# Projections with tokens as weights: 512 columns in place of 256, single weight and stage tiles, halves of the values, first heads fetched by the sync queue

## The chip, the cores and the metric

One core of one Trainium2 chip runs the kernel. The metric is the device time of one execution in microseconds (us). A core has TensorE (PE, matrix products from SBUF into PSUM; PEld is its loading of stationary operands), VectorE (DVE), ScalarE (ACT), GpSimd (POOL) and SyncE (SP); here SP does nothing but issue transfers (DMA). "SPq" and "ACTq" in a row are the queue instructions of those engines.

## The reference

One layer of a streaming encoder over 2048 tokens of width 1024, in float32.

```python
mod = silu(c) @ w_ada + b_ada                     # shifts, scales, gates: 6 x 1024
h = rmsnorm(x, g_norm1) * (1 + sc1) + sh1
q_sb, k_sb, v_sb, q_ca, k_ca, v_ca = split(h @ w_in)   # 512 columns each, 8 heads of 64
o_sb = stick_breaking_attention(q_sb, k_sb, v_sb)
o_ca = chunked_relpos_attention(rmsnorm(q_ca, g_q), rmsnorm(k_ca, g_k), v_ca, rel_bias)
x = x + gt1 * (concat(o_sb, o_ca) @ w_o)
x = x + gt2 * (relu(h2 @ w1) ** 2 @ w2)           # h2: second norm, shift and scale
```

SB names the stick-breaking heads and CA the chunked heads. CA queries and keys are normalised per head (a sum of squares over 64 columns), SB ones are not.

## The kernel before

**Products.** Each float32 operand is split into a high and a low part (`split`: ScalarE rounds a copy, another engine subtracts it from the original). A product is three matmuls (`mm3`, L202): high by high, high by low, low by high. "Stationary" is the operand that PE holds as weights, "moving" the one that streams through in columns.

**Pieces and jobs.** The 3072 columns of `w_in` are 12 pieces of 256: 0 and 1 are q_sb, 2 and 3 k_sb, 4 and 5 v_sb, 6 and 7 q_ca, 8 and 9 k_ca, 10 and 11 v_ca. Tokens are in four blocks of 512 (tb 0 to 3). A job is (f, piece, tb), where f only tells several loads of one piece apart. The startup (L437 to L506) computes the SB pieces 2, 0, 1 for block 3 in one loop over the 8 slices k of the contraction, while it computes the first columns of `mod` on VectorE (`ada_column`, L260) and normalises block 3. Then the list `jobs` (L522) is run, one after the other, by `run_job` (L538), to which the last job is left until the first attention heads' loads are issued (L1036). The SB pieces that the list lacks are projected later, during the attention (`pf` in the traces, weights `fw` read back from `scr_w`).

**Two forms of projection** (`project`, L310). For SB queries and keys the weights (128x128) are stationary and 512 tokens move; the result is tile `pq`. For CA queries and keys and all values 128 tokens of `ht` are stationary and the 256 columns of the piece move; the result is tile `pt`, and two token groups share one PSUM bank. A job of the second form is 96 matmuls. For CA it goes on with the norm per head (squares `csq` on ScalarE, sums `cv` on VectorE, the root on GpSimd), a scaled copy `qh` (VectorE), and four transposes on PE into `px`, evicted with the factor `gqk_s` into a stage tile `st` and stored to `scr_q` or `scr_k`. Values go through a stage tile `sv` to `scr_v`. Jobs of this kind are run behind their matmuls by small clocks (`Later`: a job added with n ticks runs after n PSUM groups).

**Weights** (`load_w`, L282). A raw piece (1 MB, tile `wr`, 3 buffers) is copied into `wh` by ScalarE and subtracted into `wl` by GpSimd, in eight slices; both are double buffered as whole pieces (8 slices each). `keep_w` (L305) stores them to `scr_w` for those pieces that the attention needs again.

**Norms.** `start_norm(tb, wait)` (L402) squares and adds block tb (`nsqa`, `nsaa`), and after `wait` ticks sums over partitions on PE (`pva`), takes the root, and after more ticks spreads it on PE (`pra`) and multiplies block tb by it (L412). `end_norm` (L418) applies scale and shift and splits into `ht`.

**Order.** From job 7 on (`ORDERED`) every engine keeps the order of the program text (those operations all show as line L42); between the startup and job 7 a scheduler orders ScalarE, VectorE and GpSimd. PE's order is that of the text throughout. The queue for the first attention heads' pieces is ScalarE's (`ldq = act`, L601).

Of the kernel before, what the change touches and what calls it, by code (L numbers as in the profile page):

```python
# [79 lines left out]
def encoder_kernel(ctx, tc, xT, c, g1, g2, w_in, gqk, bias, w_o, w1, w2, w_ada, b_ada, out):  # L80
# [127 lines left out]
    def store_qk(kind, ca, ps, pl, pair, tb, nm, g=None):  # L208
        st = pl.tile([P, 2, TB], F32R, tag="st", name=f"st{nm}")
# [6 lines left out]
        sp.dma_start(scr_k[at].rearrange("l d t -> d l t") if kind else scr_q[at], st.bitcast(F32))  # L216
# [21 lines left out]
    SBQK, CAQK, VALS = (2, 3, 0, 1), (6, 7, 8, 9), (4, 5, 10, 11)  # L238

    pa, er = ctx.enter_context(ExitStack()), ctx.enter_context(ExitStack())
    if True:
        xp = er.enter_context(tc.tile_pool(name="xp", bufs=KT + 2, side="right"))
        adaw = er.enter_context(tc.tile_pool(name="adaw", bufs=4, side="right"))
        adap = er.enter_context(tc.tile_pool(name="adap", bufs=1, side="right"))
# [5 lines left out]
        wp = pa.enter_context(tc.tile_pool(name="wp", bufs=2))  # L252
        ppc = er.enter_context(tc.tile_pool(name="ppC", bufs=1, space=PSUM))
        pp = Banks(zb, zb, db, zb, zb, db)

        cb = adap.tile([P, D], F32, name="cb")
        cg = adap.tile([P, D], F32, name="cg")
# [8 lines left out]
        parts = []  # L266

        def ada(j):
            wa = adaw.tile([P, D], F32, tag="wa", name=f"wa{j}")
            sp.dma_start(wa, w_ada[j * P : (j + 1) * P, :])  # L270
            behind.add(2, lambda: ada_column(j, wa))
# [5 lines left out]
        def load_raw(half, piece, q=None):  # L277
            wr = ring.tile([P, KT, CW], F32, tag="r8", name=f"wr{half}_{piece}")
            (q or sp).dma_start(wr, w_in[piece])
            return wr  # L280

        def load_w(half, piece, q=None, wr=None, parts=None):  # L282

            if wr is None:
                wr = load_raw(half, piece, q or sp)
            wh = wp.tile([P, KT, CW], F32R, tag="wh", name=f"wh{half}_{piece}")
            wl = wp.tile([P, KT, CW], F32R, tag="wl", name=f"wl{half}_{piece}")

            def low(k):
                pool.tensor_tensor(wl[:, k], wr[:, k], wh[:, k].bitcast(F32), op=ALU.subtract)  # L290

            for k in (slice(0, KT // 2), slice(KT // 2, KT)):
                act.copy(wh[:, k], wr[:, k])
                for kk in (slice(k.start, k.start + 2), slice(k.start + 2, k.stop)):
                    if parts is None:
                        low(kk)
                    else:
                        parts.append(lambda kk=kk: low(kk))
            if parts is not None:
                parts.append(lambda: behind.add(2, lambda: keep_w(half, piece, wh, wl)))  # L300
            elif q is None:
                keep_w(half, piece, wh, wl)
            return wh, wl

        def keep_w(half, piece, wh, wl):  # L305
            if half in (0, 2) and piece not in CAQK:
                for l, w in enumerate((wh, wl)):
                    sp.dma_start(scr_w[piece,][:, :, l, :], w.bitcast(F32))

        def project(piece, tb, ht, wh, wl):  # L310

            grp, hf = divmod(piece, 2)
            kind, ca = grp % 3, grp // 3
            nm = f"{piece}_{tb}"
            if not ca and kind < 2:
                for n in range(2):
                    ps = pp.tile([P, TB], F32, tag="ps", name=f"pq{nm}_{n}")
                    cl = slice(n * P, (n + 1) * P)
                    for k in range(KT):
                        mm3(ps, wh[:, k, cl], wl[:, k, cl], ht[k][:, 0, :], ht[k][:, 1, :], k == 0, k == KT - 1)  # L320
                    store_qk(kind, 0, ps, stp, hf * 2 + n, tb, f"{nm}_{n}")
                    yield
                return
            if kind < 2:
                qh = stp.tile([P, 4, CW], F32, tag="qh", name=f"qh{nm}", bufs=2)
            for t2 in range(2):
                ps = pp.tile([P, TB], F32, tag="ps", name=f"pt{nm}_{t2}")
                for tt in range(2):
                    tl = slice((2 * t2 + tt) * P, (2 * t2 + tt + 1) * P)
                    for k in range(KT):  # L330
                        mm3(
                            ps[:, tt * CW : (tt + 1) * CW], ht[k][:, 0, tl], ht[k][:, 1, tl],
                            wh[:, k, :], wl[:, k, :], k == 0, k == KT - 1,
                        )
                if kind == 2:
                    store_v(ca, ps, stp, hf, tb, t2, f"{nm}_{t2}")
                    yield
                    continue
                sq = np_.tile([P, TB], F32, tag="nsq", name=f"csq{nm}_{t2}")
                act.activation(sq, ps, AF.Square)  # L340
                v = np_.tile([P, NH], F32, tag="cv", name=f"cv{nm}_{t2}")
                dve.tensor_reduce(v, sq.rearrange("p (h d) -> p h d", d=HD), axis=AX.X, op=ALU.add)
                dve.tensor_scalar(v, v, 1.0 / HD, EPS, op0=ALU.mult, op1=ALU.add)
                y = np_.tile([P, NH], F32, tag="cy", name=f"cy{nm}_{t2}")
                t = np_.tile([P, NH], F32, tag="ct", name=f"ct{nm}_{t2}")
                rsqrt(y, v, t)
                def scale(t2=t2, ps=ps, y=y):
                    dve.tensor_tensor(
                        qh[:, 2 * t2 : 2 * t2 + 2, :].rearrange("p t (h d) -> p (t h) d", d=HD),
                        ps.rearrange("p (e d) -> p e d", d=HD),  # L350
                        y.unsqueeze(2).to_broadcast([P, NH, HD]),
                        op=ALU.mult,
                    )

                later.add(2 if osp is sp else 1, scale)
                if t2 == 1:
                    def turn(n):
                        pt = pp.tile([P, TB], F32, tag="ps", name=f"px{nm}_{n}")
                        for i in range(4):
                            pe.transpose(pt[:, i * P : (i + 1) * P], qh[:, i, n * P : (n + 1) * P], ident)  # L360
                        store_qk(
                            kind, 1, pt, stp, hf * 2 + n, tb, f"{nm}_{n}", gqk_s[:, kind : kind + 1],
                        )

                    later.add(4, lambda: turn(0))
                    later.add(4, lambda: turn(1))
                yield

        def prepare_wo(n):
# [3 lines left out]
            def rest():  # L373
                hi = stp.tile([P, KT, P], F32R, tag="st", name=f"woh{n}")
                lo = stp.tile([P, KT, P], F32R, tag="st", name=f"wol{n}")
# [4 lines left out]
            behind.add(2, rest)  # L380
# [12 lines left out]
        xts, hts, ws = {}, {}, {}  # L393
# [8 lines left out]
        def start_norm(tb, wait=3):  # L402
# [3 lines left out]
            def second():  # L406
                dg = norm_rstd(np_, pp, acc, tg)

                def third():
                    r = norm_spread(pp, dg, tg)  # L410
                    for x in xts[tb]:
                        dve.tensor_tensor(x, x, r, op=ALU.mult)  # L412
# [1204 lines left out]
```

## Time and profile before

| what | value |
|---|---|
| three executions | 2698.66, 2701.07, 2701.13 us, median 2701.07 |
| profiled execution | 2697.3 us |
| its span, from the first to the last instruction | 2695.4 us |
| mean granted TensorE clock | 0.992 |
| projections, to the first attention scores on PE | 438.6 us |

A timeline row is: start in us, duration in us, engine, line, operation, output tile <- input tiles, shape, how many in a run, and in brackets the idle time before it and what ended it. A group's row gives busy us and mean ns, or minimum, median and maximum ns of one. Matmul ends are modelled, so in a stream the distance of starts is what a matmul costs.

### The profile page before, as it was taken

What the parts mean: (1) busy time and instruction counts of PE and PEld (TensorE: products, weight loads), DVE (VectorE), ACT (ScalarE), POOL (GpSimd) and SP (SyncE); (2) the same over time, 40 slices, a digit from 0 to 9 for tenths busy, and PEclk for the clock granted to TensorE, in tenths of its full rate; (3) what the DMA queues carried; (4) which work ended last, traced back from release to release, by engine and by line L of the source; (5) the groups of instructions that cost most, each with busy time, mean ns of one, the idle gap of its engine ahead of it and who ended that gap; (6) DMA issues with size and microseconds to landing.
All of it is one profiled execution on the core that took longest, in us unless ns stands there. A gap on an engine that the chain in (4) does not pass through costs nothing. (4 is left out here: it accounts for less than half of the span.)

```text
span 2695.4 us, 42695 instructions
## 1 busy us (share of the span) xinstructions
PE 2618.6 (97%) x14192; PEld 2231.0 (83%) x14192; DVE 1881.3 (70%) x3191; ACT 1516.9 (56%) x2926; POOL 1013.1 (38%) x1264
## 2 busy tenths in 40 slices
PE   6999999899999999999999999999999999999999
PEld 5899998778778987778777888878888888888887
DVE  6435555788789978989757778767857555655565
ACT  5323444788688878878644444456544444444443
POOL 5454365576466756777522233200001323200000
PEclk9999999999999999999999999999999999999999
DMA  9869977978878688766667776786675444465574
GB/s 343 296 257 336 379 300 213 275 243 256 273 250 253 202 261 253 235 191 203 205 235 275 253 277 240 275 327 212 227 269 183 149 157 145 149 242 188 203 265 156
DMA packets 265580, 650.36 MB, mean 241 GB/s; under 512 B 29200, under 2 KB 65040, under 8 KB 255632
## 3 DMA queue, kind: packets, MB, share of 16 engines
q1 hardware_dynamic: 264576, 645.55, 70.0%
q10 hardware_dynamic: 784, 2.10, 0.3%
q8 instruction: 112, 1.84, 0.3%
q14 instruction: 108, 0.88, 0.1%
HBM read 456.16 MB, written 191.37 MB: 240 GB/s over the span
## 5 line engine op out<-in xcount | busy, mean ns | idle before, releaser
L42 PE MATMUL ps<-oph,opv 128*128 128x512 f32 x2688 | 612.3, 389 | 1.7 <-ACT opv L42 1.5
L42 PE MATMUL ps<-h,opw 128*128 128x512 f32 x2664 | 607.0, 390 | 2.2 <-DVE cx L42 2.0
L42 PEld LDWEIGHTS ps<-oph,opv 128*128 128x128 f32 x2688 | 503.8, 188 | 108.3 <-ACT opv L42 2.3
L42 PEld LDWEIGHTS ps<-h,opw 128*128 128x128 f32 x2664 | 500.3, 188 | 108.5 <-DVE cx L42 3.1
L42 POOL TENSOR_TENSOR b<-b,p 128x512 f32<-128x512 f32 (+1 forms) x320 | 359.7, 1124 | 188.3 <-DVE p L42 167.8
L42 DVE TENSOR_TENSOR wtl<-wt,wth 128x512 fp32r<-128x512 f32 (+3 forms) x544 | 289.9, 544 | 50.4 <-ACT wth L42 48.1
L42 ACT CAST wth<-wt 128x512 fp32r<-128x512 f32 (+3 forms) x544 | 257.6, 484 | 115.2 <-PE wt L42 99.6
L42 DVE TENSOR_TENSOR oph<-hw,oph 128x512 fp32r<-128x512 f32 x224 | 156.1, 697 | 220.3 <-ACT oph L42 220.3
L42 PE MATMUL pt<-wh,ht 128*128 128x256 f32 x1664 | 304.3, 284 | 1.7 <-DVE qh L42 1.7
L42 POOL TENSOR_TENSOR ts<-w 128x512 f32<-128x512 f32 x32 | 44.9, 1403 | 681.5 <-DMA w<-in_w_dram 310.0
L42 ACT CAST oph<-hw 128x512 fp32r<-128x512 f32 x224 | 139.3, 622 | 282.8 <-PE ps L42 267.3
L42 DVE TENSOR_TENSOR_SCAN p<-z,p,zero 128x512 f32<-128x512 f32 x192 | 245.9, 1281 | 34.1 <-ACT z L42 28.9
L42 PEld LDWEIGHTS pt<-wh,ht 128*128 128x128 f32 x1664 | 260.8, 192 | 1.9 <-ACT st L42 1.9
L42 PE MATMUL pt<-wl,ht 128*128 128x256 f32 x832 | 235.3, 283 | 0.0
L42 PE MATMUL acc<-wth,v 128*128 128x512 f32 (+3 forms) x544 | 223.0, 414 | 0.0
L42 ACT ACTIVATE b<-z 128x512 f32<-128x512 f32 (+1 forms) x320 | 171.6, 536 | 63.2 <-PE z L42 45.9
L42 POOL TENSOR_TENSOR e<-e,cols 128x640 f32<-128x640 f32 (+4 forms) x128 | 143.0, 1121 | 145.6 <-DVE cols L42 86.7
L42 PE MATMUL z<-k,q 128*128 128x512 f32 (+3 forms) x640 | 186.3, 373 | 9.9 <-DVE p L42 7.2
L42 PE MATMUL acc<-wtl,v 128*128 128x512 f32 (+3 forms) x544 | 187.1, 350 | 0.0
L42 PE MATMUL wt<-ident,b 128*128 128x128 f32 x1088 | 173.3, 275 | 6.7 <-DVE cols L42 5.1
L42 DVE TENSOR_TENSOR opw<-w,opw 128x512 fp32r<-128x512 f32 x127 | 100.4, 793 | 112.7 <-ACT opw L42 112.6
L42 ACT ACTIVATE z<-z 128x512 f32<-128x512 f32 (+1 forms) x320 | 170.7, 533 | 0.0
(222 smaller groups left out, 4644.5 us busy)
## 6 DMA issues: line engine op xcount, KB each, us to landing
hw<-scr_hid SPq DMA_DIRECT2D x112, 512.0 KB, 4.0
v<-scr_v SPq DMA_DIRECT2D x136, 256.0 KB, 3.8
k<-scr_k SPq DMA_DIRECT2D x268, 128.0 KB, 4.1
w<-in_w_dram SPq DMA_DIRECT2D x64, 512.0 KB, 5.2
hw<-scr_s SPq DMA_DIRECT2D x64, 512.0 KB, 4.7
q<-scr_q SPq DMA_DIRECT2D x124, 256.0 KB, 5.2
fw<-scr_w SPq DMA_DIRECT2D x28, 1024.0 KB, 7.0
wa<-in_w_ada_dram SPq DMA_DIRECT2D x48, 512.0 KB, 7.0
```

The lines of the kernel that those rows point to most:

```text
L42: return lambda *x, **y: self.tc.keep_in_program_order(f(*x, **y))
```

## The change

- Pieces from 4 on are taken in pairs, 512 columns at once (`w_rest`, a second view of `w_in` made on the host). 128 tokens are stationary as before and 512 columns move; one token group fills one PSUM bank. The banks are now four for projections (`pp`) and two for norms and transposes (`pq`).
- Split weights lie in nine single tiles, each the high and low part of one slice of 512 columns (or two slices of 256). The low part is made by VectorE in place of GpSimd. During the last token group of a key `pump` refills each tile after PE's last use of it.
- Staging is six single tiles `st`; a value group is written as two halves of 256 columns, two token groups to a store. `qh` is six tiles of 128x512. The scale that writes it runs two projections later (`scale_last`), and the four transposes of a job come 3 and 4 groups later.
- `start_norm` multiplies by the learned scale as well (one instruction a slice), and `end_norm` adds the shift on ScalarE and makes the low part on VectorE: 8 and 8 instructions, where it was 16 and 8. Its position for block 2 is two groups later.
- All engines and SP keep the order of the text from the start on.
- The list of jobs is new (below); piece 3 for block 2 is loaded and split once more.
- `gqk` is loaded behind the first six stores and scaled on VectorE after the first half of (0,3,3); pieces 2 and 3 are stored to `scr_w` by ScalarE's queue.
- The last job is (1,4,1) with 512 columns; `ldq` is SP's queue in program order.

```diff
-        VALS = (4, 5, 10, 11)
+    CAQK, VALS = (6, 8), (4, 10)
+    WT = 9
...
-            dve.tensor_tensor_reduce(cb, wa, cs, 1.0, bcol[:, j : j + 1], ALU.mult, ALU.add, m)
+            dve.tensor_tensor_reduce(wa, wa, cs, 1.0, bcol[:, j : j + 1], ALU.mult, ALU.add, m)
...
+        def weight_parts(key, m):
+            f, p = key
+            w = w_tile(f"{f}_{p}_{m}")
+            wts.setdefault(key, []).append(w)
...
+            split(hi, lo, src)
...
+        def pump():
+            while coming and free[0]:
+                weight_parts(*coming.pop(0))
+        def scale_last():
+            for x in scales:
+                x[0] += 1
+            while scales and scales[0][0] == 2:
+                scales.pop(0)[1]()
...
-            for t2 in range(2):
-                ps = pp.tile([P, TB], F32, tag="ps", name=f"pt{nm}_{t2}")
-                for tt in range(2):
-                    tl = slice((2 * t2 + tt) * P, (2 * t2 + tt + 1) * P)
-                    for k in range(KT):
-                        mm3(
-                            ps[:, tt * CW : (tt + 1) * CW], ht[k][:, 0, tl], ht[k][:, 1, tl],
-                            wh[:, k, :], wl[:, k, :], k == 0, k == KT - 1,
-                        )
+            for tt in range(4):
+                ps = pp.tile([P, TB], F32, tag="ps", name=f"pt{nm}_{tt}")
+                tl = slice(tt * P, (tt + 1) * P)
+                if last and tt == 3:
+                    pump()
+                for k in range(KT):
+                    mm3(ps, ht[k][:, 0, tl], ht[k][:, 1, tl], *weight_of(key, k), k == 0, k == KT - 1)
+                    if last and tt == 3:
+                        free[0] += 1
+                        pump()
+                scale_last()
...
-                    for x in xts[tb]:
-                        dve.tensor_tensor(x, x, r, op=ALU.mult)
+                    for k, x in enumerate(xts[tb]):
+                        dve.scalar_tensor_tensor(x, x, aff[:, 0, k : k + 1], r, op0=ALU.mult, op1=ALU.mult)
...
-                norm_apply(0, xts[tb][k], k, ht, np_, f"a{tb}")
+                b = mod[:, k : k + 1]
+                act.activation(ht[k][:, 0, :], x, AF.Identity, bias=b)
+                dve.scalar_tensor_tensor(
+                    ht[k][:, 1, :], x, b, ht[k][:, 0, :].bitcast(F32), op0=ALU.add, op1=ALU.subtract
+                )
...
-        jobs = [(0, 3, 3), (0, 6, 3), (0, 3, 2), (0, 6, 2), (2, 2, 2), (0, 0, 2), (0, 1, 2)]
-        jobs += [(0, p, t) for p in seq[5:10] for t in (3, 2)]
-        jobs += [(0, 10, 3), (0, 11, 3), (0, 10, 2), (0, 11, 2)]
-        jobs += [(1, p, t) for p, t in ((4, 1), (6, 1), (7, 1), (6, 0), (7, 0), (8, 1), (8, 0), (9, 1), (9, 0), (5, 1))]
+        jobs = [(0, 3, 3), (0, 6, 3), (0, 6, 2), (2, 3, 2), (2, 2, 2), (0, 8, 3), (0, 8, 2), (2, 0, 2), (2, 1, 2)]
+        jobs += [(0, p, t) for p in (4, 10) for t in (3, 2)]
+        jobs += [(1, p, t) for p, t in ((6, 1), (6, 0), (8, 1), (8, 0), (4, 1))]
...
-        start_norm(2, 1)
+        start_norm(2, 2, 2)
...
-        ldq = act
+        ldq = osp
```

Three places show how instructions move. In the rows a name carries piece, block and group (`pq0_3_3_1` is f 0, piece 3, block 3, second half; `pt0_6_3_0` f 0, piece 6, block 3, token group 0).

PE's order at the end of (0,3,3) and the start of (0,6,3), before:

```order
L42 MATMUL pq3_3_0_759<-ht3_7_397,wh0_3_674 128x512 x2
L42 MATMUL pq3_3_0_759<-ht3_7_397,wl0_3_675 128x512
L42 MATMUL pva2_788<-ones_261,nsaa2_726 128x1 x4
L42 MATMUL pq3_3_1_804<-ht3_0_390,wh0_3_674 128x512 x2
L42 MATMUL pq3_3_1_804<-ht3_0_390,wl0_3_675 128x512
```

And PE's order there after:

```order
L42 MATMUL pq0_3_3_1_785<-ht3_5_392,w0_3_2_673 128x512 x3
L42 MATMUL pq0_3_3_1_785<-ht3_6_393,w0_3_3_676 128x512 x3
L42 MATMUL pq0_3_3_1_785<-ht3_7_394,w0_3_3_676 128x512 x3
L42 MATMUL pva2_838<-ones_261,nsaa2_729 128x1 x4
L42 MATMUL pt0_6_3_0_858<-w0_6_0_786,ht3_0_387 128x512 x3
L42 MATMUL pt0_6_3_0_858<-w0_6_1_789,ht3_1_388 128x512 x3
```

The sum over partitions for block 2 (`pva2`) stood between the two halves of (0,3,3); it now stands behind the second half, ahead of (0,6,3), whose matmuls read one weight tile for each slice.

VectorE's order around the end of the norm of block 2, where `xt2` and `ht2` are that block, `cv` the sums of a CA norm and `qh` the scaled copy, before:

```order
L412 TENSOR_TENSOR xt2_7_696<-xt2_7_696,pra2_833 128x512
L148 TENSOR_TENSOR ht2_981<-xt2_0_682,ht2_981 128x512
L148 TENSOR_TENSOR ht2_981<-xt2_1_684,ht2_981 128x512
L342 TENSOR_REDUCE cv6_3_0_900<-csq6_3_0_898 128x8
L148 TENSOR_TENSOR ht2_981<-xt2_2_686,ht2_981 128x512
L343 TENSOR_SCALAR cv6_3_0_900<-cv6_3_0_900 128x8
```

And VectorE's order there after:

```order
L42 SCALAR_TENSOR_TENSOR ht2_951<-xt2_6_618,mod_271,ht2_951 128x512
L42 SCALAR_TENSOR_TENSOR ht2_951<-xt2_7_620,mod_271,ht2_951 128x512
L42 TENSOR_TENSOR qh0_6_3_0_993<-pt0_6_3_0_858,cy0_6_3_0_888 128x512
L42 TENSOR_REDUCE cv0_6_3_2_997<-csq0_6_3_2_995 128x8
L42 TENSOR_SCALAR cv0_6_3_2_997<-cv0_6_3_2_997 128x8
L42 TENSOR_TENSOR qh0_6_3_1_1034<-pt0_6_3_1_899,cy0_6_3_1_929 128x512
```

The scaled copies were mixed in among the norm's instructions by the scheduler; the first one now stands behind all sixteen of them.

ScalarE's order at the start of the attention, where `b0_0_3_3_0` is the first work on attention scores, before:

```order
L42 CAST sv5_1_0_4953<-pt5_1_0_4904 128x8x64
L42 ACTIVATE st9_1_0_4962<-px9_1_0_4957,gqk_s_269 128x512
L42 ACTIVATE st9_1_1_4971<-px9_1_1_4966,gqk_s_269 128x512
L42 CAST sv5_1_1_5025<-pt5_1_1_4976 128x8x64
L42 ACTIVATE st9_0_0_5038<-px9_0_0_5033,gqk_s_269 128x512
L42 ACTIVATE st9_0_1_5047<-px9_0_1_5042,gqk_s_269 128x512
L42 ACTIVATE b0_0_3_3_0_5083<-z0_0_3_3_0_5029 128x512
```

And ScalarE's order there after:

```order
L42 ACTIVATE st1_8_0_2_3897<-px1_8_0_2_3892,gqk_s_269 128x512
L42 ACTIVATE st1_8_0_3_3906<-px1_8_0_3_3901,gqk_s_269 128x512
L42 CAST sv1_4_1_2_0_3886<-pt1_4_1_3_3910 128x4x64
L42 CAST sv1_4_1_2_1_3887<-pt1_4_1_3_3910 128x4x64
L42 ACTIVATE b0_0_3_3_0_3977<-z0_0_3_3_0_3941 128x512
```

The evictions of the last keys (`st`) stood between the last value's copy and the first scores; they now stand ahead of the last value group's copies. The loads of the first heads, which stood in this queue earlier, are on SP.

More of the change, by code (lines that the diff above doesn't have):

```diff
@@ L305, in keep_w, with load_raw @@
[L305 to L315, printed above, removed]
+        raws, wts, free = {}, {}, [WT]
+        def load_raw(key, m, q=None):
+            p = key[1]
+            if p < 4:
+                raws[key, 0] = ring.tile([P, KT, CW], F32, tag="r8", name=f"wr{key[0]}_{p}")
+                src = w_in[p]
+            else:
+                raws[key, m] = ring.tile([P, KT // 2, TB], F32, tag="r8", name=f"wr{key[0]}_{p}_{m}")
+                src = w_rest[p // 2 - 2][:, m * KT // 2 : (m + 1) * KT // 2, :]
+            (q or sp).dma_start(raws[key, m], src)
@@ L578, in run_job @@
                     credit -= cost
+            for _ in bank:
+                pass
+            assert not coming
         for n in range(len(jobs) - 1):
             run_job(n)
-        while parts:
-            parts.pop(0)()
         for _, job in todo:
```

258 lines of the change are left out of this document (142 added, 116 removed).

## Prediction

> **What bounds the kernel now.** I read the page's busy times and its chain first, then the windows of the part that the diff touches, then TensorE's waits and its timeline there.
>
> ```profile
> PE 2618.6 (97%) x14192; PEld 2231.0 (83%) x14192; DVE 1881.3 (70%) x3191; ACT 1516.9 (56%) x2926; POOL 1013.1 (38%) x1264
> ...
> PE 33%; DVE 1%; ACT 0%; DMA 0%; issue 0%; SPq 0%; DVEq 0%
> ```
>
> TensorE (PE) is busy 97% of the span, and nearly all that the chain names is PE. So a change counts by the matmul time it removes and by the PE waits it removes or makes. The windows (from, to, then busy time of PE, PEld, DVE, ACT, POOL, PE's granted clock, DMA share, GB/s):
>
> ```profile
> 40.00:80.00 40.00, 37.86 (x172) 31.71 (x171) 23.20 (x37) 21.18 (x37) 18.08 (x18) 0.91 0.91 336
> ...
> 200.00:300.00 100.00, 100.00 (x839) 100.00 (x839) 55.53 (x81) 35.02 (x53) 34.45 (x46) 1.00 0.95 350
> 300.00:440.00 140.00, 138.35 (x1160) 137.86 (x1158) 74.36 (x126) 53.97 (x82) 74.63 (x116) 1.00 0.81 294
> ```
>
> The projections end near 438 us. From 80 us on, PE is full. Its waits between 80 and 440 us are one single row:
>
> ```profile
> PE pt L42 <- DVE qh L42: 1.7, 1, 1.7
> ```
>
> The attention and the MLP behind it keep their code and their matmuls; I cost them at nothing, and give the shifted transfers at the seam a share of the range. Three things are left to cost: matmuls, the hole near 64 us, and the seam at 438 us.
>
> **A: 512 columns instead of 256.** TensorE's timeline, first SB keys (three 512-column matmuls a product), then CA queries (three of 256):
>
> ```profile
> 140.06 0.61 PE L42 MATMUL pq<-ht,wh 128*128 128x512 f32 x2
> 140.51 0.39 PE L42 MATMUL pq<-ht,wl 128*128 128x512 f32 x1
> ...
> 144.82 0.61 PE L42 MATMUL pq<-ht,wh 128*128 128x512 f32 x2
> ```
> ```profile
> 150.05 0.40 PE L42 MATMUL pt<-wh,ht 128*128 128x256 f32 x2
> ...
> 162.29 0.40 PE L42 MATMUL pt<-wh,ht 128*128 128x256 f32 x2
> ```
>
> Read the starts, as ends are modelled. 140.06 to 144.82 is 7 products: 0.68 us each, 226.7 ns a matmul. 150.05 to 162.29 is 34: 0.36 us, 120 ns a matmul. Two narrow matmuls take 240 ns, one wide 226.7: some 13 ns are paid for each matmul and not for its columns, and the wide form pays them half as often. How many there are, from the rows of the tile pt (1664 + 832 matmuls), and whether a wide matmul costs the same with another stationary operand, from the page's largest group:
>
> ```profile
> L42 PE MATMUL pt<-wh,ht x1664: 277/283/365, 77.1 to 438.5; 128*128 128x256 f32 x185
> ...
> L42 PE MATMUL pt<-wl,ht x832: 280/283/283, 77.3 to 438.4; 128*128 128x256 f32 x167
> ```
> ```profile
> L42 PE MATMUL ps<-oph,opv 128*128 128x512 f32 x2688 | 612.3, 389 | 1.7 <-ACT opv L42 1.5
> ```
>
> 612.3 / 2688 is 227.8 ns, so yes. 832 products become 416: 832 × 0.36 − 416 × 0.68 = 299.5 − 282.9 = **16.6 us** less, all on the bound engine. The form itself (tokens stationary, 512 moving) is not in this trace; its bounds are 0.72 for the wide product (gain 0) and 0.68. I take 0.68, which two unlike forms show. The Trainium skill, page "TensorE: Matmul & The Clock Gate", section "Wait — 56ns, not 53.3ns?", puts the fixed cost of a warm matmul at about 2.5 ns; by it this term would be 1248 × 2.5 ns, an estimate of 3.1 us. The rows above disagree.
>
> **B: the hole near 64 us.** TensorE, then VectorE, then the same step in a warm place, then all seven of VectorE's adds (min/median/max ns):
>
> ```profile
> 58.84 0.62 PE L42 MATMUL pq<-ht,wh 128*128 128x512 f32 x2
> ...
> 64.06 0.39 PE L42 MATMUL pq<-ht,wl 128*128 128x512 f32 x1
> 66.58 1.86 PE L42 MATMUL pva<-ones,nsaa 128*128 128x1 f32 x8 [2.14 <-DVE nsaa L168]
> 68.31 1.20 PE L42 MATMUL pq<-ht,wh 128*128 128x512 f32 x2
> ...
> 76.25 1.06 PE L42 MATMUL pra<-ndga,ones 128*128 128x128 f32 x8
> ```
> ```profile
> 60.60 2.27 DVE L168 TENSOR_TENSOR nsaa<-nsaa,nsqa 128x512 f32<-128x512 f32 x3
> 63.50 3.03 DVE L168 TENSOR_TENSOR nsaa<-nsaa,nsqa 128x512 f32<-128x512 f32 x2 [0.63 <-ACT nsqa L167]
> ```
> ```profile
> 248.57 0.95 PE L42 MATMUL pva<-ones,nsaa 128*128 128x1 f32 x8
> 249.38 0.36 PE L42 MATMUL pt<-wh,ht 128*128 128x256 f32 x1
> ```
> ```profile
> L168 DVE TENSOR_TENSOR nsaa<-nsaa,nsqa x7: 681/693/1566, 53.0 to 65.0; 128x512 f32<-128x512 f32 x7
> ```
>
> The first half of (0,3,3) runs 58.84 to 64.28 (8 × 0.68); the norm's sums are late, and the second half starts at 68.31: 4.03 us, of which 0.81 is the step itself when warm (249.38 − 248.57). The second half takes 76.25 − 68.31 = 7.94 instead of 5.44, at a lower granted clock (0.91 for the window). Now pva2 stands behind both halves, 5.44 us later, while the sums need some 2.3 us: the hole goes. 4.03 + 2.50 − 0.81 = **5.7 us** less. Next late are the splits of (0,6): behind the first half's store VectorE now scales g_q and g_k, whose load was issued at 41 us and is now behind the six stores (the last four of which SP issued from 58.86 on).
>
> ```profile
> 41.26 0.42 SPq L42 DMA_DIRECT2D gqk_sb<-in_gqk_dram  x1
> ...
> 58.86 3.32 SPq L216 DMA_DIRECT2D scr_q<-st  x4
> ```
> ```profile
> gqk_sb<-in_gqk_dram SPq DMA_DIRECT2D x1, 1.0 KB, 5.8
> ...
> 77.68 4.86 DVE L412 TENSOR_TENSOR xt<-xt,pra 128x512 f32<-128x512 f32 x8
> ```
>
> 5.8 us after an issue near 62 us is 68; then the first split (0.61 each by the second row), against a need at 70.5 (58.84 + 10.88 + 0.81). Cost 0 to 4; I take **+0.5**.
>
> **C: the wait for qh.** One gap, and PE at full speed right behind it (371.18 to 374.42 is 9 products of 0.36):
>
> ```profile
> 370.87 0.36 PE L42 MATMUL pt<-wh,ht 128*128 128x256 f32 x1 [1.65 <-DVE qh L42]
> ...
> 371.18 0.40 PE L42 MATMUL pt<-wh,ht 128*128 128x256 f32 x2
> ...
> 374.42 0.40 PE L42 MATMUL pt<-wh,ht 128*128 128x256 f32 x2
> ```
>
> It is the second PSUM group of (1,7,0), counting jobs of 11.5 us back from 438.6; that job is no longer in the list: **−1.65**, bounds 0 and −1.65. Its place is taken by two others, below.
>
> **D: the seam at 438 us.** ScalarE and TensorE:
>
> ```profile
> 439.78 1.26 ACT L42 ACTIVATE st<-px,gqk_s 128x512 fp32r<-128x512 f32 x2 [0.40 <-PE px L42]
> ```
> ```profile
> 441.31 0.44 PE L42 MATMUL z<-k,q 128*128 128x128 f32 x2 [0.34 <-DVE st L42]
> ...
> 443.33 0.73 PE L42 MATMUL z<-k,q 128*128 128x512 f32 x2 [1.51 <-DVE p L42]
> ```
>
> The last key heads' evictions stand ahead of the first scores', 1.26 us on ScalarE, and PE waits 0.34 + 1.51. Now the turns lie inside (1,4,1), and ScalarE meets the first scores at once. Gain 0 to 1.85; I take **−1.2**.
>
> **What is added.** After each norm for a CA block VectorE has 16 instructions (8 scale, 8 low parts) ahead of the first qh scale:
>
> ```profile
> L42 DVE SCALAR_TENSOR_TENSOR st<-px,gqk_s,st 128x512 fp32r<-128x512 f32 x26 | 18.2, 743 | 0.0
> ```
>
> At 0.66 between 0.61 and 0.74 that is 10.6 us, and 0.69 for the scale. Two PSUM groups of 5.44 lie between that point and the fifth group, which needs the first bank back: short by 0.4 plus the latencies. I take +1.6 at (0,6,2) and +1.0 at (1,6,0), **+2.6**, bounds 0 and 5.
>
> The low parts leave GpSimd:
>
> ```profile
> L42 POOL TENSOR_TENSOR wl<-wr,wh 128x512 fp32r<-128x512 f32 x48 | 63.2, 1339 | 77.2 <-DMA b<-in_bias_dram 30.6 <-ACT wh L42 26.4 <-DMA scr_v<-sv 20.1
> ...
> L290 POOL TENSOR_TENSOR wl<-wr,wh 128x512 fp32r<-128x512 f32 x24 | 32.1, 1367 | 26.3 <-ACT wh L293 26.3
> ```
>
> 72 of them, and 4 for (2,3) once more, at 0.61 put 46 us on VectorE over some 380: its 55.5% (200 to 300 us) becomes 68%. At each of the 11 changes of weights 8 such parts, 4.9 us, must follow the tiles that PE frees through the last 5.44 us; part k is needed 5.44 us after its tile came free, and copy plus subtraction take about 1.2. PE's last group hides it; VectorE's other work may take up to 3 or 4 us there. Cost **0**, and each excess is paid in full.
>
> The queues were busy when V ran:
>
> ```profile
> DMA packets 11726, 19.26 MB, mean 385 GB/s; under 512 B 479, under 2 KB 9543, under 8 KB 11337
> ```
>
> That is 250 to 300 us, without a PE wait. The four V jobs of 21.8 us now carry 31.4 MB by the sizes on the queues: 361 GB/s. Six stage tiles and three raw halves wait for those stores. **+1.5**, bounds 0 and 6.
>
> **Sum.** −16.6 − 5.7 − 1.65 − 1.2 + 0.5 + 2.6 + 1.5 = −20.5. The profiled execution took 2697.3 (span 2695.4): 2676.8. It lies 3.8 under the median 2701.07; at the median's level the forecast is **2680.5**.
>
> **Rivals.** The queues from 300 to 400 us:
>
> ```profile
> DMA packets 11367, 32.99 MB, mean 330 GB/s; under 512 B 877, under 2 KB 5308, under 8 KB 10461
> ```
>
> 1. *The V jobs are bound by transfers.* For: 0.95 DMA share. Against: no PE wait there. At the 330 GB/s of the next 100 us the 31.4 MB need 95 us where PE has 87: with the other terms 2680.5 + 8 − 1.5 = **2687**; with late raw halves for CA too, up to 2694.
> 2. *The fixed price does not halve*, because it belongs to columns or to loading the tokens: A is 0, **2697**, within 0.2% of 2701. Against: 227.8 ns in the MLP. With the page's 2.5 ns instead, A is 3.1 and the time about 2694.
> 3. *Slower: single tiles stall PE at each change of weights.* If VectorE's queue holds a part back by 2.14 us, as the sums did at 64 us, and PE cools as it did there (2.50), 11 × 4.64 = 51: **2731**. Without cooling 11 × 2.14 = 23.5: 2704. It decides from 20.5 / 11 = 1.9 us a change. For: no second buffer. Against: 3 us of slack. The Trainium skill, same page, section "What's actually happening", has the clock fall after an idle window of about 3.4 us: by that, pauses of 2 us would stay warm (the 1.7 us one at 369 us was followed by full speed), and 4 us would not, as at 64 us.
>
> **How the numbers follow.** Forecast 0.72, rival 1 0.17, rival 2 0.05, rival 3 0.06. Low end: gains at their bounds without costs, −25.8 or 2675, less the 2.4 between the runs' median and their lowest (2698.66), and some 4 for a seam that happens to fall better: 2669. High end: rival 1's bad side, 2693. A measurement of this kernel tells 0.2% (5.4 us) from no change; faster takes the forecast and nearly all of rival 1 (0.87), same is rival 2 and the rest of 1 (0.07), slower rival 3 (0.06).
>
> **What would show it.** pt products 0.68 apart, with 1248 matmuls; no PE gap between 64 and 77 us and a granted clock near 1.0 in 60 to 80; PE waits "pt <- DVE qh" of 1 to 2 us, twice; the attention's first scores some 19 us earlier than now (−16.6 − 5.7 − 1.65, and +4.6). I am wrong if PE waits for w tiles (rival 3), for sv stages or raw halves (rival 1), or if the triples stand 0.72 apart (rival 2).

## The result, and the profile after

The changed kernel takes **2685.5 us** (median of five, 2683.0 to 2686.8) against 2701.07 of the kernel before: ratio 0.9942, 95% interval 0.9928 to 0.9955. That is 15.6 us less; the interval goes from 12 to 19. The forecast was 2680.5 within 2669 to 2693. A second set of the same two kernels, below, gave 0.9931 (0.9915 to 0.9946).

The profiled execution took 2683.0 us, its span 2681.1, where the kernel before had 2697.3 and 2695.4. Its page, busy times and the chain that ended last:

```profile
PE 2600.1 (97%) x12944; PEld 2162.3 (81%) x12944; DVE 1919.8 (72%) x3287; ACT 1510.9 (56%) x2962; POOL 921.3 (34%) x1192
...
PE 33%; DMA 1%; DVE 1%; ACT 0%; issue 0%; POOL 0%; SPq 0%; DVEq 0%; ACTq 0%
```

PE has 1248 matmuls fewer, which is the halving of pt, and 18.5 us less busy time. The windows of the projections, with the columns as before:

```profile
40.00:80.00 40.00, 39.22 (x177) 32.31 (x177) 27.32 (x47) 24.41 (x44) 8.14 (x12) 1.00 1.03 395
...
200.00:300.00 100.00, 100.00 (x459) 83.13 (x458) 61.23 (x105) 40.33 (x79) 2.38 (x9) 1.00 1.00 369
300.00:420.00 120.00, 118.89 (x565) 99.11 (x564) 82.02 (x145) 42.74 (x76) 44.05 (x92) 1.00 0.77 283
```

The granted clock between 40 and 80 us is 1.00 where it was 0.91. In 200 to 300 us the DMA engines are full and PE still never waits. Then TensorE's waits from 60 to 430 us, all of them:

```profile
PE pt L42 <- DVE qh L42: 2.2, 2, 1.1
PE z L42 <- DVE p L42: 1.2, 1, 1.2
PE pt L42 <- DVE w L42: 0.8, 1, 0.8
PE z L42 <- DVE sv L42: 0.5, 1, 0.5
```

The two waits for qh are those that the forecast had put after the two norms. The one for w was half a microsecond in the forecast. The last row and the second one are the seam to the attention. TensorE's timeline at the start and at the seam:

```profile
59.57 11.04 PE L42 MATMUL pq<-ht,w 128*128 128x512 f32 x48
70.45 0.95 PE L42 MATMUL pva<-ones,nsaa 128*128 128x1 f32 x8
71.26 0.48 PE L42 MATMUL pt<-w,ht 128*128 128x512 f32 x1
72.52 10.99 PE L42 MATMUL pt<-w,ht 128*128 128x512 f32 x47 [0.78 <-DVE w L42]
83.35 1.06 PE L42 MATMUL pra<-ndga,ones 128*128 128x128 f32 x8
```
```profile
414.65 1.03 PE L42 MATMUL px<-ident,qh 128*128 128x128 f32 x8
415.44 5.70 PE L42 MATMUL pt<-w,ht 128*128 128x512 f32 x24
420.98 0.61 PE L42 MATMUL z<-k,q 128*128 128x512 f32 x2
...
423.02 0.41 PE L42 MATMUL z<-k,q 128*128 128x128 f32 x2 [0.52 <-DVE sv L42]
...
424.72 0.73 PE L42 MATMUL z<-k,q 128*128 128x512 f32 x2 [1.22 <-DVE p L42]
```

Both halves of (0,3,3) now run without a hole, 59.57 to 70.45 (48 × 226.7 ns). The first scores start at 420.98 where they started at 438.60: 17.6 us earlier, though this execution reached 59.57 where the other was at 58.84. At the fifth pair of score matmuls the lead is 443.33 − 424.72 = 18.6. At the end of the span it is 14.3. So there are two questions: what each part of the 18.6 is, and where the 4.3 behind it went.

### The profile page after: what moved, and what is told of

Same layout as the page of the kernel before. It is cut to its first block, busy times and chain, and to the rows that moved or that the text cites. A ratio compares the mean times of both kernels' runs of the same rounds, so it can differ in the third digit from the quotient of the medians.

```text
span 2681.1 us, 40293 instructions
## 1 busy us (share of the span) xinstructions
PE 2600.1 (97%) x12944; PEld 2162.3 (81%) x12944; DVE 1919.8 (72%) x3287; ACT 1510.9 (56%) x2962; POOL 921.3 (34%) x1192
## 5 line engine op out<-in xcount | busy, mean ns | idle before, releaser
L42 PE MATMUL pt<-w,ht 128*128 128x512 f32 x1248 | 289.0, 391 | 2.9 <-DVE qh L42 2.2
L42 PEld LDWEIGHTS pt<-w,ht 128*128 128x128 f32 x1248 | 232.8, 188 | 51.6 <-ACT csq L42 2.9
L42 PE MATMUL po<-fx,ow 128*128 128x512 f32 x576 | 166.4, 404 | 6.0 <-DMA ow<-scr_wo 6.0
```

The costliest lines, as they stand in the source:

```text
L42: return lambda *x, **y: self.tc.keep_in_program_order(f(*x, **y))
```

## The experiments

Each kernel below is the changed kernel with one edit, unless it says otherwise. The times are medians of the kernel and the ratio to the kernel before, measured in turn on one chip within a set. Kernels that stand in one set shared the runs of the kernel before.

| run | set | median us | ratio to the kernel before, 95% interval |
|---|---|---|---|
| e0, unaltered | 1 | 2683.3 | 0.9931 (0.9915 to 0.9946) |
| e1, two halves | 1 | 2698.9 | 0.9991 (0.9981 to 1.0002) |
| e2, norm early | 1 | 2688.4 | 0.9954 (0.9938 to 0.9970) |
| e3, g_q and g_k early | 1 | 2682.2 | 0.9933 (0.9917 to 0.9948) |
| e4, heads by ScalarE | 2 | 2687.4 | 0.9952 (0.9937 to 0.9968) |
| e5, scale early | 2 | 2682.1 | 0.9924 (0.9908 to 0.9939) |
| e6, low parts on GpSimd | 2 | 2703.5 | 1.0007 (0.9996 to 1.0017) |
| e7, e3 and e5 | 2 | 2680.5 | 0.9923 (0.9908 to 0.9939) |
| e8, turns late | 3 | 2688.4 | 0.9953 (0.9940 to 0.9965) |
| e9, e7 and first scores early | 3 | 2679.1 | 0.9915 (0.9901 to 0.9929) |
| e10, eight tiles | 3 | 2680.1 | 0.9928 (0.9915 to 0.9940) |
| e11, the kernel before | 4 | 2702.1 | 1.0005 (0.9991 to 1.0018) |

Each set ran on a chip of its own, so kernels of different sets are compared by their ratios. A median's interval here is 3 to 4 us wide on each side. Effects of 1 to 3 us are therefore read from the trace, between two marks on PE: the first pt matmul (71.26 in the changed kernel) and the attention's first scores (420.98). That stretch is 349.72 us in the changed kernel and 348.72 in e0, the same kernel, where PE had no wait for w (the reason stands under e3). A kernel whose profile lacks that wait is compared with 348.72.

**e1: is it the number of matmuls?**

```diff
-                    mm3(ps, ht[k][:, 0, tl], ht[k][:, 1, tl], *weight_of(key, k), k == 0, k == KT - 1)
+                    for c in range(2):
+                        cc = slice(c * CW, (c + 1) * CW)
+                        wk = [w[:, cc] for w in weight_of(key, k)]
+                        mm3(ps[:, cc], ht[k][:, 0, tl], ht[k][:, 1, tl], *wk, k == 0, k == KT - 1, more=True)
```

> Each wide product with tokens stationary is made as two of 256 columns into the two halves of the same bank; all else is as in the changed kernel. Theory (13.3 ns are paid per matmul whatever its columns): 1248 matmuls more, 1248 x 13.3 ns = 16.6 us longer than the changed kernel, 2702 us; spacing in pt 120 ns. Rival (the time goes by columns and the gain came from elsewhere): no change, 2685.5. Rival by the 2.5 ns a matmul of the page on TensorE: 3.1 us longer, 2688.6.

This kernel makes all the matmuls, but it begins the two halves of a bank in turn, and the sums that come out of pt are not the projection; only its time is used. The tile pt in it, then TensorE's two marks:

```profile
L42 PE MATMUL pt<-w,ht x2496: 277/283/420, 70.9 to 436.8; 128*128 128x256 f32 x192
```
```profile
70.86 0.36 PE L42 MATMUL pt<-w,ht 128*128 128x256 f32 x1
...
436.92 0.63 PE L42 MATMUL z<-k,q 128*128 128x512 f32 x2
```

The stretch is 366.06 us, 16.3 more than 349.72, against 16.6 forecast; the median of e1 is 15.6 over that of e0. With the same engines, tiles, transfers and order and the columns unchanged, 1248 matmuls more cost 13.1 ns each. Two other differences in this profile pull opposite ways. From 73.1 to 76.5 us PE had a granted clock of 0.50, which costs about 1.7 us, and its two waits for qh are 1.0 us in all, not 2.2. Without both some 15.8 us are left, 12.7 ns a matmul. A price by columns alone would give 0, so that rival falls. Not separated is what the price belongs to: every matmul comes with a load of its stationary operand (PE and PEld have 14192 instructions each in e1 and 12944 each in the changed kernel), so it is the price of the pair.

The Trainium skill, page "TensorE: Matmul & The Clock Gate", section "Wait — 56ns, not 53.3ns?", gives about 2.5 ns for each warm matmul; for 1248 of them that is an estimate of 3.1 us, and the 16.3 us measured here disagree with it.

**e2: did the place of the norm make the hole?**

```diff
-        start_norm(2, 2, 2)
+        start_norm(2, 1, 3)
```

> The sum over partitions for block 2 is put back between the two halves of (0,3,3); the spreading stays where it is. Theory (its place made the hole): the sums end at 66.8 us, PE reaches the place at 65.0 and idles about 2 us, and the second half runs cold as before (2.5 us more): 4 us longer than the changed kernel, 2689.5; the 0.8 us wait for the weights of (0,6) vanishes under it. Rival (the low parts of weights on GpSimd slowed VectorE's sums, and with those gone the place does not matter): within 0.5 us of 2685.5, no idle PE before pva.

TensorE and VectorE in e2:

```profile
61.17 5.60 PE L42 MATMUL pq<-ht,w 128*128 128x512 f32 x24
68.57 1.05 PE L42 MATMUL pva<-ones,nsaa 128*128 128x1 f32 x8 [1.80 <-DVE nsaa L42]
69.49 7.34 PE L42 MATMUL pq<-ht,w 128*128 128x512 f32 x24
76.66 1.52 PE L42 MATMUL pt<-w,ht 128*128 128x512 f32 x6
```
```profile
63.05 5.47 DVE L42 TENSOR_TENSOR nsaa<-nsaa,nsqa 128x512 f32<-128x512 f32 x7 [0.36 <-ACT nsqa L42]
```

The hole is back, with 1.80 us of idle PE, and the second half takes 7.17 us (69.49 to 76.66) where the first took 5.44. GpSimd makes no low parts here, and the seven sums take the same 5.47 us as in the changed kernel. So the place matters, and the rival falls. From the start of (0,3,3) to the first pt matmul e2 needs 15.5 us where the changed kernel needs 11.7; the 0.78 us for w is then gone, and to the first scores at 425.22 it is 364.05 us against 361.41, so 2.6 are left by the trace. The forecast of 4 had the second half as slow as before the change (2.5 us lost, where it is 1.7). The granted clock was 0.50 for 3.4 us behind the hole in e2 (69.7 to 73.1) and for 6.8 us in the kernel before (66.6 to 73.4). The medians differ by 5.1, with intervals that overlap a little.

**e3: the load of g_q and g_k.** It is issued ahead of raw piece 3 and removed from behind the stores:

```diff
+                osp.dma_start(gqk_sb, gqk)
                 load_raw(*loads.pop(0), osp)
...
-        osp.dma_start(gqk_sb, gqk)
```

> The load of g_q and g_k is issued as in the kernel before, ahead of the raw piece 3 near 42 us. Theory (VectorE waited 4.14 us for this transfer and the weights of (0,6) stood behind that): VectorE begins the splits of (0,6) at 67.5 us in place of 71.8, PE's wait of 0.78 us for w at 72.5 is gone, and the first matmul's late start with it: 1.0 us shorter in the profile, 2684.5. Rival (the raw half of (0,6) or VectorE's queue would have been late anyway): the wait stays, 2685.5.

VectorE in the changed kernel, then in e3:

```profile
66.83 0.68 DVE L42 TENSOR_TENSOR st<-pq,st 128x512 fp32r<-128x512 f32 x1
71.65 0.15 DVE L42 TENSOR_SCALAR gqk_s<-gqk_sb 128x1 f32<-128x1 f32 x1 [4.14 <-DMA gqk_sb<-in_gqk_dram]
71.72 0.14 DVE L42 COPY gqk_s<-gqk_sb 128x1 f32<-128x1 f32 x1
71.78 4.89 DVE L42 TENSOR_TENSOR w<-wr,w 128x512 fp32r<-128x512 f32 x8
```
```profile
66.73 0.68 DVE L42 TENSOR_TENSOR st<-pq,st 128x512 fp32r<-128x512 f32 x1
67.33 0.14 DVE L42 TENSOR_SCALAR gqk_s<-gqk_sb 128x1 f32<-128x1 f32 x1
67.39 0.14 DVE L42 COPY gqk_s<-gqk_sb 128x1 f32<-128x1 f32 x1
67.45 4.90 DVE L42 TENSOR_TENSOR w<-wr,w 128x512 fp32r<-128x512 f32 x8
```

A transfer of 1 KB, issued at 64.68 behind the stores, held VectorE for 4.14 us, and eight weight parts behind it. In e3 they start at 67.45 and PE does not wait. The stretch between the marks is 348.71 us, 1.01 less; the theory had 1.0. The median cannot show this (2682.2 against 2683.3). Nor does every execution pay it. In the unaltered e0 VectorE waited 0.76 us for the same transfer, PE did not wait for w, and the stretch is 348.72. So e3 removes a cost of 1.0 us that the profiles of the changed kernel, e1, e8 and e10 show and those of e0, e4 and e5 do not.

**e4: the queue of the first heads' pieces.**

```diff
-        ldq = osp
+        ldq = act
```

> The first heads' pieces are fetched by ScalarE's queue again; all else as in the changed kernel. Theory (which queue issues them is of no weight for PE: the attention, from its first scores to its last output copy, took 944.4 to 946.1 us in the changed kernel's profiles and 944.9 in the kernel before): within 1 us of the changed kernel, whose executions centre on 2684; the same stretch between 944 and 946.5. Rival (on SP the loads stand behind stores, and that is what the seam lacks against the forecast): 1.5 to 3 us shorter, with fewer waits of cz for scr_k.

TensorE's wait, then ScalarE's rows in e4:

```profile
PE px L42 <- DVE qh L42: 2.4, 1, 2.4
```
```profile
399.66 1.34 ACTq L42 DMA_DIRECT2D q<-scr_q  x2
405.49 1.78 ACTq L42 DMA_DIRECT2D k<-scr_k  x2
407.37 0.37 ACT L42 CAST sv<-pt 128x256 fp32r<-128x256 f32 x1 [10.18 <-DMA k<-scr_k]
```

My theory falls here. Issuing the loads held ScalarE for 10.18 us while it had a value group to copy; VectorE's subtraction of that group waits for the copy, a scale of qh stands behind it, and the transposes on PE wait 2.4 us. The rival does not hold either: the loads of the first scores were not what the seam lacks. By the trace the stretch is 351.33 us. PE did not wait for w here, so it is 2.6 longer than in e0, nearly all of it this wait. The attention, from its first scores to its last output copy, took 942.2 us, less than the 944 to 946.5 that the theory had; but its waits of cz for scr_k are 5.9 us, not fewer. The kernel before had the same kind of stall on ScalarE without a wait of PE; in the new order there is one. ScalarE in the kernel before:

```profile
432.71 0.59 ACT L42 CAST sv<-pt 128x512 fp32r<-128x512 f32 x1 [5.70 <-DMA k<-scr_k]
```

So keeping these loads on SP is worth 2.6 us in this order, and I had given it nothing.

**e5 and e7: the waits after the norms.** The first scale of (0,6,3) and (1,6,1) runs one group earlier; e7 has e3's edit as well.

```diff
-                scales.append([0, scale])
+                scales.append([int((f, piece, tb, tt) in ((0, 6, 3, 0), (1, 6, 1, 0))), scale])
```

> The first qh scale of (0,6,3) and of (1,6,1) is put one token group earlier, ahead of the sixteen instructions of the norm. Theory (the bank waits for that scale only): both waits of pt for qh (1.04 and 1.11 us) are gone with the slow matmul behind each, 2.4 us shorter than the changed kernel, 2681.5. Rival (the scale would wait for GpSimd's root and hold the norm back, so that PE waits for ht instead): PE waits for ht or w in its place, no gain.

> The early load of g_q and g_k and the early scale together. Theory: both waits are separate, 1.0 + 2.4 = 3.4 us shorter than the changed kernel, 2680.5, and no PE wait is left between 60 us and the attention. Rival: one of the two only uncovers another wait, and the sum is less than 2.

VectorE in the changed kernel (the wait's cause), then all of TensorE's waits from 57 to 440 us in e7:

```profile
84.98 5.35 DVE L42 SCALAR_TENSOR_TENSOR xt<-xt,aff,pra 128x512 f32<-128x512 f32 x8
90.25 5.38 DVE L42 SCALAR_TENSOR_TENSOR ht<-xt,mod,ht 128x512 fp32r<-128x512 f32 x8
95.55 0.68 DVE L42 TENSOR_TENSOR qh<-pt,cy 128x512 f32<-128x512 f32 x1
```
```profile
PE z L42 <- DVE p L42: 1.5, 2, 1.2
PE z L42 <- DVE sv L42: 0.5, 1, 0.5
```

The sixteen instructions take 10.6 us, as worked out, and the scale stood behind them. With it ahead, no wait is left before the attention. Between the marks e5 has 346.03 us and e7 346.00, 3.7 less than the changed kernel, against 3.4 forecast for e7. In the profile of e5 the transfer of g_q and g_k landed early enough (70.40 us, not 71.65) that PE did not wait for w, as in e0; against e0's 348.72 the early scale alone is worth 2.7. Both theories hold; between these marks e7's profile is no shorter than e5's, where the transfer happened to land in time. e7's ratio is 0.9923.

**e6 and e10: is there slack at the changes of weights?**

```diff
-            split(hi, lo, src)
+            split(hi, lo, src, pool)
```

> The low parts of the weights behind the startup are made by GpSimd again, all else as in the changed kernel. Theory (the single tiles live on VectorE's 0.61 us a part; a GpSimd part takes 1.34): 8 parts take 10.7 us where PE's last group and the first one of the next key cover 10.2 and GpSimd also makes the roots of the CA norms, so PE waits 1 to 4 us at each of the seven changes to a key of 8 parts: 7 to 28 us longer, I take 15, 2699; waits of pt for w on POOL. Rival (the changes of weights have slack to spare): under 2 us longer.

```diff
-    WT = 9
+    WT = 8
```

> Eight single weight tiles in place of nine; all else as in the changed kernel. Theory (a part is needed 5.4 us after its tile came free and takes 1.2): each part may come 0.68 us later without a wait of PE, 2684, within 1 us of the changed kernel. Rival (the changes of weights run without slack): up to 0.68 us at each of eleven changes, 7 us longer, 2691, with waits of pt for w.

GpSimd's and TensorE's rows in e6, VectorE's for the same parts in the changed kernel, and TensorE's only wait for w in e10:

```profile
L42 POOL TENSOR_TENSOR w<-wr,w 128x512 fp32r<-128x512 f32 x72 | 92.2, 1319 | 74.0 <-DMA wa<-in_w_ada_dram 37.0 <-ACT w L42 36.5 <-POOL b L42 0.6
```
```profile
PE pt L42 <- POOL w L42: 8.8, 28, 0.7
```
```profile
L42 DVE TENSOR_TENSOR w<-wr,w 128x512 fp32r<-128x512 f32 x72 | 44.2, 683 | 0.2
```
```profile
PE pt L42 <- DVE w L42: 1.1, 1, 1.1
```

On GpSimd a part takes more than twice as long, PE stops 28 times for at most 0.7 us, and the stretch grows by 16.8 us (366.48); in the median the gain of the whole change is gone. The size is near the 15 us expected, the form is not: many short stops, 8.8 us in all, and slower matmuls around each, in place of 1 to 4 us at seven changes. On VectorE one tile fewer costs nothing: e10's only wait for w (its stretch is 350.10 us) stands where VectorE waited 4.44 us for g_q and g_k. So rival 3 named a real danger. The 0.61 us of VectorE's stream (44.2 / 72) is what keeps it away, and there is at least one tile of slack.

**e8 and e9: the seam.** e8 leaves the last keys' turns behind the first scores. e9 is e7 with the first scores and their chain ahead of the last value group.

```diff
-                        later.add(3 + n // 2, lambda n=n: turn(n))
+                        later.add(99 if (f, piece, tb) == (1, 8, 0) else 3 + n // 2, lambda n=n: turn(n))
```

> The four turns (16 transposes and their evictions) of the last keys, (1,8,0), are left until behind the first scores, as the kernel before had its last two. Theory (they stand between ScalarE and the first scores there): the last value matmul to the fifth score matmul pair grows from 3.7 us in the changed kernel by 1.6 us of transposes and about 1 us of ScalarE's evictions beyond PE's, while (1,4,1) gets 1.6 us shorter: about 1 us longer in all, 2685. Rival (the seam's wait is set by something else, so it comes to nothing): the two 1.6 us cancel, 2684.

```diff
                 hook(jobs[n], b)
+                if n + 1 == len(jobs) and b == 3:
+                    units[0].scores(0)
+                    units[0].soft1(0)
                 next(bank)
...
-        units[0].scores(0)
         later.flush()
...
-            if front is not None:
+            if front is not None and i:
                 front.soft1(fs)
```

> The early load of g_q and g_k and the early scale, and the first head's first scores with their ScalarE, VectorE and GpSimd work put ahead of the last value group's matmuls. Theory (in the changed kernel PE waits 0.52 + 1.22 us because the first scores' chain only starts behind the last values' copies): both waits go, 1.2 to 1.7 us shorter than with the two early steps alone, and PE no longer runs cold for 1.55 us in some executions: 2678.5. Rival (the last values' copies are then late and the first scores of the next steps wait instead): no gain over 2680.5.

TensorE in e8, then in e9:

```profile
420.48 1.04 PE L42 MATMUL px<-ident,qh 128*128 128x128 f32 x8
422.82 1.31 PE L42 MATMUL px<-ident,qh 128*128 128x128 f32 x8 [1.30 <-DVE st L42]
...
427.19 0.73 PE L42 MATMUL z<-k,q 128*128 128x512 f32 x2 [1.98 <-DVE p L42]
```
```profile
410.85 1.03 PE L42 MATMUL px<-ident,qh 128*128 128x128 f32 x8
411.64 0.71 PE L42 MATMUL z<-k,q 128*128 128x512 f32 x2
...
419.78 0.70 PE L42 MATMUL z<-k,q 128*128 128x512 f32 x2 [0.75 <-PE z L42]
```

From the first pt matmul (71.92 in its profile) to the fifth score pair e8 takes 355.3 us, the changed kernel 353.5: 1.8 longer, where about 1 was expected. The turns do stand in the way of the first scores. In e9 the stretch from the last turns' transposes to the fifth pair is 8.93 us (410.85 to 419.78); in the changed kernel it is 10.07 (414.65 to 424.72). That is 1.1 less, just under the forecast of 1.2 to 1.7; 0.75 us of waiting is left, now for a score matmul's own chain. e9 is the quickest of all at **2679.1 us, 0.9915 (0.9901 to 0.9929)**, below both kernels. Its lead over e7 lies inside the intervals.

**e0 and e11: where are the 4.3 us?** Both kernels once more, unaltered.

> The changed kernel once more, unaltered, as the level for the runs beside it. Both theories: 2685.5 us, within 2 of it; the profile shows again where the spread of the profiled executions lies (start of the attention's first scores at 421.0 us, the MLP's waits behind 1450 us). If the first scores stand at 421.0 within 0.3 and the end moves by 2 or more, what the forecast lacks behind 500 us is scatter and not the change.

> The kernel before once more, unaltered, for a second profile of it. Question: from the fifth score matmul pair on the changed kernel lost 4.3 us of the 18.6 it had gained by then. Theory (the first profile of the kernel before was a quick execution, 3.8 us under the median, and this lay in the attention and the MLP, whose times scatter): the projections end at 438.6 within 1 us, and from there to the end it takes 2259 to 2262 us in place of 2256.8. Rival (the change makes the same attention and MLP slower, by transfers that now collide): again 2256 to 2258 us, where the changed kernel's two profiles have 2260.2 and 2260.7; and the waits of pf and cz for their loads in the first 260 us of the attention stay at 3.6 and 3.1 us.

The first matmuls of TensorE's filler work behind the fifth score pair: first the changed kernel, then e0:

```profile
425.33 3.21 PE L42 MATMUL pf<-ht,fw 128*128 128x512 f32 x7
```
```profile
426.09 1.86 PE L42 MATMUL pf<-ht,fw 128*128 128x512 f32 x7
```

Same program, same waits in front (0.52 and 1.22 us in both): in one execution the seven matmuls run at a granted clock of 0.53 and 1.3 us are lost, in the other at 1.00. That explains 1.3 of the 4.3. What had been set for e0 was not met: its first scores stand at 421.73, not within 0.3 of 421.0, because PE reached (0,3,3) 1.75 us later, and its span is 1.3 longer, not 2 or more. The attention behind it, from its first to its last output copy, takes 922.5 and 922.6 us in the two profiles of the kernel before, 923.2 and 923.3 in the two of the changed one. From there to the end it is 1311.9 and 1312.2 before, 1314.0 and 1316.0 after, and 1312.9 to 1320.1 over the other ten. So the rest, 2 to 4 us, lies in the out-projection and the MLP, whose code and instructions are the same.

The granted clock shows more of it. PE and the other engines over 100 us from the last output copy on, first the kernel before, then the changed one (the columns are those of the windows above):

```profile
1383.40:1483.40 100.00, 90.47 (x381) 72.82 (x380) 64.69 (x91) 39.50 (x64) 19.22 (x13) 0.97 0.76 274
```
```profile
1367.10:1467.10 100.00, 90.41 (x369) 72.38 (x369) 62.82 (x89) 38.03 (x62) 19.48 (x13) 0.93 0.76 269
```

PE is busy for as long, but at a clock of 0.93 in place of 0.97 it makes 12 matmuls fewer. The second profiles agree: 0.97 in e11, 0.93 in e0. PE's waits behind the last output copy are no longer than before: 13.0 us in the kernel before and 12.5 in e11, 11.5 and 12.9 in the two of the changed one. Over all fourteen profiles the part behind the last output copy takes 1311.9 to 1314.6 us in the five with 0.97 in these 100 us (e3, e6 and e7 among them, which have the changed kernel's code here) and 1313.4 to 1320.1 us in the nine with 0.95 or 0.93. So the missing time goes with a lower granted clock rather than with longer waits.

My theory for e11 (2259 to 2262 us from the first scores to the end) fell: it was 2257.1, as in the first profile. The rival's mechanism holds by half: the waits of cz for scr_k are 4.9 us in e11, not 3.1, against 5.0 and 4.0 after, so they are scatter; those of pf for fw are 3.7 again, against 5.6 and 6.5 after. But that is in the attention, which is only 0.7 us longer in all, and not where the time is missing. Both profiled executions of the kernel before lie 4 us under the medians (2697.3 and 2698.0 against 2701.1 and 2702.1), those of the changed kernel do not (2683.0 and 2684.2 against 2685.5 and 2683.3). Why the clock was lower for longer in both profiles of the changed kernel, and whether its executions mostly pay these 2 us, stays open. The lead of 18.6 us before it lies inside both intervals of the whole (12 to 19 and 15 to 23).

## Why the prediction was right, and what was off in it

The time fell by the mechanism that was named, and most terms of the sum have the size that was given. Point by point:

- **A, −16.6.** Right. 1248 matmuls fewer; undone alone, 16.3 on the trace and 15.6 in the median (e1). The pt matmuls are busy for 304.25 us in the kernel before and 288.18 in e7, where none of them waits: 16.1. The step that took 0.68 us from two other forms of matmul carried over to the form that the trace had not shown.
- **B, −5.7.** Right. From the start of (0,3,3) to the first pt matmul 18.22 us became 11.69, of which 0.81 is pra, which only moved: 5.7. Putting the norm back (e2) costs 3.8 of it on the same stretch. The other 1.9 is about what the longer slow clock took in the kernel before (6.8 us at 0.50 against 3.4).
- **C, −1.65.** Gone, as said.
- **Waits after the norms, +2.6.** Right: 1.04 and 1.11 us of idle, 2.4 with the slow matmul behind each; e5 is 2.7 shorter without them.
- **g_q and g_k, +0.5.** Mis-sized: 1.0 in this profile, and 0 in some others (e0). The cause was named; the landing took 7 us behind the stores, not 5.8, and was issued 2.7 us later than assumed.
- **V jobs and their transfers, +1.5.** Nothing. The DMA engines were full from 200 to 300 us, and PE did not wait once. Rival 1 did not occur.
- **Changes of weights, 0.** Right, by e10; by e6 it depends on VectorE making the low parts.
- **D, the seam, −1.2.** This step failed. From the first scores to the fifth pair 4.73 us became 3.74. But 0.79 of the 4.73 were transposes that had only been moved into (1,4,1) and are paid there; I had not counted them. What is left is 0.2, because the last values' copies took the place of the keys' evictions: PE waits 0.52 + 1.22 where it waited 0.34 + 1.51. The prediction asked "what is late next" elsewhere and not here.
- **The queue of the first heads, nothing.** Against the kernel before it is no gain, since PE did not wait there; but it keeps a wait of 2.4 us out of the new order (e4), which I had not seen.

With A at its even pace and the 2.7 of e5 for the waits, the terms are −16.6 − 5.7 − 1.65 − 0.2 + 1.0 + 2.7 = −20.45. This execution also came 0.7 us later out of the startup, which makes 19.7; the trace shows 18.6 at the fifth score pair. The 1.1 between them is in the distances of the matmuls, summed over the stage: with the waits left out, pt stand some 0.7 and pq and px some 0.4 us more above their even pace than in the kernel before, which the sum had not counted. So at this point the forecast was 1.9 us too high, and the missing 1.0 in D is the largest term of that. It was luck that the error is not larger: the V jobs' 1.5 that never came hid as much again. Behind this point 1.3 us were a slow clock that not every execution has, and about 2 us more went with a lower granted clock in the MLP, whose cause is open.

## What to carry to other kernels

On a PE that never waits, count matmuls: at a fixed number of columns each one fewer, with its load of the stationary operand, was worth about 13 ns here, and halving their number moved the kernel by about that product. When work is moved off the seam between two stages, book it where it lands, and ask which instruction is now the last ahead of the next stage's first one. An engine's queue that issues a load or waits for one, however small, holds all that stands behind it: 1 KB cost VectorE 4 us, and loads on ScalarE 10.

## What the runs showed of the hardware

- A pause of 1.80 us with a short norm step around it (66.6 to 69.5 us in e2) was followed by 24 matmuls in 7.17 us in place of 5.44, at a granted clock of 0.50 for 3.4 us. In the kernel before PE had idled 2.14 us at this place, not the 4 us that the prediction's third rival took for the pause, and the clock was 0.50 for 6.8 us.
- Waits of 0.52 and 1.22 us within 3.7 us at the seam were followed by a clock of 0.50 from 425.5 to 428.9 us in the changed kernel's profile and by 1.00 in e0's. The ten profiles with this order at the seam all have these two waits (0.5 and 1.2 us); behind them the clock fell in five (the changed kernel, e1, e3, e4, e10) and stayed at 1.00 in five.
- Two waits of 1.04 and 1.11 us in a stream left the clock at 1.00 and cost one slow matmul each (0.31 us) and no more.
- The Trainium skill, page "TensorE: Matmul & The Clock Gate", section "What's actually happening", has a free-running window of about 3.4 us behind the clock. The stretches of 3.4 us at 0.50 and the two outcomes of one program at the seam agree with that. The pauses of 1.80 and 2.14 us are shorter than such a window and were still followed by a slow clock.
- The same subtraction of 128x512 takes 0.61 us in VectorE's stream (44.2 / 72) and 1.28 in GpSimd's (92.2 / 72).
